# A hybrid decoder layer on one core: where u is scaled, where the SSM answers are split, and when small transfers are issued

## The chip, the core and the metric

The kernel runs on one NeuronCore of a Trainium2 chip. The metric is the device time of one execution in microseconds (us), median of three runs. Engines are named as in the profile: PE (TensorE matmul), PEld (its weight loads), DVE (VectorE), ACT (ScalarE), POOL (GpSimd), SP (SyncE, which here only issues DMAs; SPq and ACTq are the queues of DMA issues on SP and ACT).

## The reference

One decoder layer on x of 2048 tokens by 1024 channels, float32. The input is normalised by RMSNorm and multiplied by one matrix `w_in`; the columns go to three mixers:

- A, sliding-window attention with 4 heads and learned sinks (window 128);
- B, a complex diagonal state space model (SSM, "S5"): 32 groups of 16 channels, 64 complex states a group, a scan over time, then `GELU(Re(C s) + D u)`, then a gated linear unit: `ab = z @ glu_w + glu_b`, `out = ab[:512] * sigmoid(ab[512:])`;
- C, native sparse attention with compressed, selected and window branches.

The three outputs are normalised, projected by `w_out` and added to x; then a feed-forward block `x + w_down @ relu(w_up @ RMSNorm(x))^2` is added.

## The kernel before

Products in float32 precision are made from three fast products: each operand is split into a high word rounded to `fp32r` (an ACT cast) and the rest (a DVE or POOL subtraction), and `mm3` (L80) adds high x high, high x low and low x high in PSUM.

**Stages.** `phase_front` (L93) does the normalisation and `w_in` in two halves of the tokens (8 row tiles each). In each half it first makes `u` for all four 128-channel blocks in two groups of four row tiles (`u_step`, L156), then the column chunks a, b, c (`product`, L170), each with its 8 weight tiles loaded by `load_w` (L153), 2 raw buffers and 12 split ones. Norm factors are not known when the products start: `row_sum` (L112) loads x row-wise and sums squares; `row_factors` (L117) makes 1/rms in `rx` and **stores the [128 x 8] tile transposed to DRAM (`rx_d`, L121)**: 1024 single 4-byte values. In half 0 the front also computes the SSM's parameter tables (`ssm_tables`, L327, a generator run in steps: `TABLE_PARTS = (8, 4)`; its second block, L432 on, loads C, B and D into a pool that opens after the first one has closed) and stores per-pair tables (`pair_steps`). In half 1 the SSM itself is interleaved with the products of a, b, c (`ssm_steps`, L551): for each of 16 pairs of groups it loads u and tables (`loaded`, two pairs ahead), multiplies u by the row factors of both halves (`scaled`, one DVE product of 128x512), multiplies, scans (`scanned`) and answers (`answer`), where GELU leaves `z`; ACT casts it (L627), POOL subtracts (L628), and both words are stored (`stored`, L630).

**Order.** The front is placed by the framework's scheduler: each engine's list is ordered by program order as a priority among what the scheduler thinks ready, and on the chip each engine and each DMA queue runs its list in order. After the front, the local stage and all that follows are ordered by a planner in the kernel (`Flow`, L878): tasks ask for an engine with an estimated duration and a rank, and the planner writes the lists.

**Local stage.** Sliding-window attention (`Local`) runs at high rank; the GLU's 16 row tiles (`glu_tasks`, L2073) run at low rank beside it. For a row tile, `rows_of` (L707) loads both words of z in four DMAs of 128 KB, three tiles ahead (`ZBUFS`); `part` multiplies. The GLU's bias rows are fetched by a task `bias` (L2131) on SP in the planner's order, then cast by ACT (L699) and split by DVE (L703).

Of the kernel before, what the change touches and what calls it, by code (L numbers as in the profile page):

```python
# [92 lines left out]
def phase_front(tc, C, x, norm1_g, w_in, uT, pd, rh_a, prm, ssm_d, rx_d, consts, extra, later, x_t, r_last, last_bank):  # L93

    nc = tc.nc
    with ExitStack() as ctx:
# [56 lines left out]
        def load_w(half, kind, c0, n):  # L153
            return [keep_w(half, kind, c0, n, k, fetch_w(half, kind, c0, n, k, sp, 2, nc.sync)) for k in range(NK)]

        def u_step(half, j, k, hs, w, banks, pool):  # L156
            hh, hl = hs
            for f in range(4):
# [39 lines left out]
        for half in range(2):  # L198
# [10 lines left out]
            if half:  # L209
                tables = table_steps(tc, C, S, ctx.enter_context(tc.tile_pool(name="sgt", bufs=1, side="right", reuse_waits="tile")), ps_t)  # L210
            c_x = ctx.enter_context(ExitStack())
            with tc.tile_pool(name=f"a_psu{half}", bufs=1, space=PSUM, reuse_waits="tile") as ps_u:
                xp = c_x.enter_context(tc.tile_pool(name=f"a_x{half}", bufs=3, **({} if half else {"reuse_waits": "tile"})))
                c_o = ctx.enter_context(ExitStack())
                box_x[:] = [xp, c_o.enter_context(tc.tile_pool(name=f"a_o{half}", bufs=4, side="right", reuse_waits="tile"))]
                banks, parts = {}, []
# [22 lines left out]
                if half == 0:  # L239
# [5 lines left out]
                    run(merge(second, sums[0], [lambda: next(gen)] * TABLE_PARTS[0]))  # L245
# [3 lines left out]
            if half == 0:  # L249
                with tc.tile_pool(name="sg_ps0", bufs=1, space=PSUM, reuse_waits="tile") as ps_g:  # L250
                    l2 = lists[0]
# [75 lines left out]
def ssm_tables(tc, C, S, pool, prm, dkp):  # L327
# [20 lines left out]
    with ExitStack() as ctx:  # L348
        tp = ctx.enter_context(tc.tile_pool(name="si", bufs=1))
        sc = tmp([P, 2, 11, G], "sc")  # L350
        sn, cs = sc[:, 0], sc[:, 1]

        ar, ai, ldt = tmp([P, G], "ar"), tmp([P, G], "ai"), tmp([P, G], "ldt")
        nc.sync.dma_start(ldt, log_dt[0:1].to_broadcast([P, G]))
        for src, dst in ((a_re, ar), (a_im, ai)):
            for j in range(2):
                nc.sync.dma_start(dst[64 * j:64 * j + 64], src)
        dt = exp_acc(nc, tp, ldt, [P, G], "e1")

        yield  # L360
        jt = C["ramp"]
        xr = tmp([P, 17, G], "xr")
        adr, adi = tmp([P, G], "adr"), tmp([P, G], "adi")
        nc.vector.tensor_tensor(adr, ar, dt, op=ALU.mult)
        nc.vector.tensor_tensor(adi, ai, dt, op=ALU.mult)
        nc.vector.tensor_tensor(xr, adr.unsqueeze(1).broadcast_to([P, 17, G]), jt.unsqueeze(2).broadcast_to([P, 17, G]), op=ALU.mult)
        yield
        rho = exp_acc(nc, tp, xr, [P, 17, G], "e2")
        yield
        nc.vector.tensor_copy(rho16, rho[:, 16])  # L370
        yield
        th = tmp([P, 11, G], "th")
        for j in range(11):
            nc.vector.tensor_scalar(th[:, j], adi, float(2 ** j), None, op0=ALU.mult)
        sincos(nc, tp, sc, th, [P, 11, G], "sc")

        yield
        pr, pi_ = (tp.tile([P, 17, G], F32, tag="e2" + n, name="t_p" + n) for n in ("xc", "r"))
        t1, t2 = tmp([P, 8, G], "t1"), tmp([P, 8, G], "t2")
        nc.vector.memset(pr[:, 0], 1.0)  # L380
        nc.vector.memset(pi_[:, 0], 0.0)
        for j in range(4):
            n = 2 ** j
            er = cs[:, j:j + 1].broadcast_to([P, n, G])
            ei = sn[:, j:j + 1].broadcast_to([P, n, G])
            nc.vector.tensor_tensor(t1[:, :n], pr[:, :n], er, op=ALU.mult)
            nc.vector.tensor_tensor(t2[:, :n], pi_[:, :n], ei, op=ALU.mult)
            nc.vector.tensor_tensor(pr[:, n:2 * n], t1[:, :n], t2[:, :n], op=ALU.subtract)
            nc.vector.tensor_tensor(t1[:, :n], pr[:, :n], ei, op=ALU.mult)
            nc.vector.tensor_tensor(t2[:, :n], pi_[:, :n], er, op=ALU.mult)  # L390
            nc.vector.tensor_tensor(pi_[:, n:2 * n], t1[:, :n], t2[:, :n], op=ALU.add)
        nc.vector.tensor_copy(pr[:, 16], cs[:, 4])
        nc.vector.tensor_copy(pi_[:, 16], sn[:, 4])
        nc.vector.tensor_tensor(AR, pr, rho, op=ALU.mult)
        nc.vector.tensor_tensor(AI, pi_, rho, op=ALU.mult)
# [554 lines left out]
def cast_ns(n):  # L950
    return 197 + 0.72 * n
# [1971 lines left out]
```

## Time and profile before

| | us |
|---|---|
| median of 3 runs (2460.09 to 2462.77) | 2462.41 |
| the profiled execution: time | 2462.57 |
| the profiled execution: span | 2460.8 |

The span is what the trace shows; 1.8 us lie around it. PE is busy 96% of the span. A number such as "x85" is a count of instructions; in a list of waits, "idle" is the time that an engine stood just before an instruction, and the name behind the arrow is what ended it. PEclk is the granted TensorE clock as a share of its upper level: 1.00 is 2.4 GHz, 0.50 is 1.2 GHz, and a value between is a mix over the stretch.

### The profile page before, as it was taken

The numbers are of one execution on the slowest core, as the hardware profiler recorded it, in microseconds if no ns is written. First come the engines' busy times: TensorE is split into PE (matmuls) and PEld (weight loads), VectorE is DVE, ScalarE is ACT, GpSimd is POOL, SyncE is SP. The second block draws the span as 40 slices with busy tenths as digits, with TensorE's granted clock in tenths as the row PEclk, the third lists the DMA queues.
The fourth block names the chain that finished last, engine by engine and source line by source line (L and its number), as shares of the span: only waits on it lengthen the run. The fifth ranks groups of instructions, "written<-read, shape, count | busy, mean of one in ns | idle before, by whom it ended". The sixth has DMA issues, their size and how long they took to land. (4 is left out here: it accounts for less than half of the span.)

```text
span 2460.8 us, 37124 instructions
## 1 busy us (share of the span) xinstructions
PE 2367.4 (96%) x12290; PEld 2027.0 (82%) x12290; DVE 1775.2 (72%) x3463; ACT 1302.2 (53%) x2736; POOL 1048.5 (43%) x1080
## 2 busy tenths in 40 slices
PE   8799989799899999999999999999999999999999
PEld 6788989687788888888888888888887888888887
DVE  7764894675687788888665556745558888889886
ACT  5344444675677667666565556444444444434442
POOL 0000243232334345331667664665563544455547
PEclk9799999899999999999999999999999999999999
DMA  8466555563322243210657668654548443444435
GB/s 250 130 216 186 182 180 176 127 214 106 104 87 83 70 123 117 70 54 33 214 182 210 188 193 257 191 155 146 161 146 283 130 125 106 125 133 133 130 99 196
DMA packets 432529, 369.71 MB, mean 150 GB/s; under 512 B 47014, under 2 KB 387244, under 8 KB 430256
## 3 DMA queue, kind: packets, MB, share of 16 engines
q1 hardware_dynamic: 376912, 325.50, 43.6%
q10 hardware_dynamic: 55424, 41.84, 5.4%
q8 instruction: 97, 1.59, 0.3%
q14 instruction: 96, 0.79, 0.1%
HBM read 240.11 MB, written 132.35 MB: 151 GB/s over the span
## 5 line engine op out<-in xcount | busy, mean ns | idle before, releaser
L2180 ACT CAST v<-vr 128x512 fp32r<-128x512 f32 x224 | 139.2, 623 | 303.7 <-DMA vr<-vd 147.0
L2181 DVE TENSOR_TENSOR v<-vr,v 128x512 fp32r<-128x512 f32 x224 | 234.9, 1056 | 76.5 <-ACT v L2180 75.3
L2344 DVE TENSOR_TENSOR ul<-fs,uh 128x512 fp32r<-128x512 f32 x124 | 113.4, 934 | 109.1 <-ACT uh L2343 109.1
L2642 PE MATMUL pdc<-dw,v 128*128 128x512 f32 x768 | 186.4, 392 | 5.2 <-ACT dw L2180 3.9
L2642 PE MATMUL pdb<-dw,v 128*128 128x512 f32 x768 | 184.5, 389 | 0.0
L2642 PE MATMUL pda<-dw,v 128*128 128x512 f32 x768 | 184.5, 389 | 0.0
L2642 PEld LDWEIGHTS pdc<-dw,v 128*128 128x128 f32 x768 | 144.8, 189 | 36.7 <-ACT dw L2180 4.3
L2642 PEld LDWEIGHTS pdb<-dw,v 128*128 128x128 f32 x768 | 144.1, 188 | 30.0
L2642 PEld LDWEIGHTS pda<-dw,v 128*128 128x128 f32 x768 | 144.1, 188 | 29.9
L613 POOL TENSOR_TENSOR t<-Q,E 128x508 f32<-128x508 f32 x16 | 24.5, 1532 | 334.7 <-DMA CA<-dca 273.1
L2343 ACT CAST uh<-fs 128x512 fp32r<-128x512 f32 x124 | 74.4, 620 | 162.3 <-POOL fs L2332 132.6
L2344 DVE TENSOR_TENSOR ul<-ur,uh 128x512 fp32r<-128x512 f32 x93 | 88.7, 955 | 67.9 <-ACT uh L2343 66.4
L2491 POOL TENSOR_TENSOR ev<-ex,e 128x512 f32<-128x512 f32 x32 | 43.2, 1349 | 209.4 <-ACT ex L2474 209.4
L1611 ACT CAST ths<-pps 128x512 fp32r<-128x512 f32 (+1 forms) x144 | 79.2, 562 | 72.4 <-PE pps L1595 63.3
L2474 ACT ACTIVATE e<-e 128x512 f32<-128x512 f32 x128 | 81.0, 633 | 62.3 <-DVE e L2443 60.3
L1938 PE MATMUL pw<-wo_h,mh 128*128 128x512 f32 x256 | 106.6, 416 | 3.2 <-DVE mx L1960 3.1
L1616 DVE TENSOR_TENSOR tls<-pps,ths 128x512 fp32r<-128x512 f32 (+1 forms) x144 | 93.0, 657 | 20.9 <-ACT ths L1611 19.4
L1938 PE MATMUL pw<-wo_l,mh 128*128 128x512 f32 x256 | 104.0, 406 | 0.0
L1938 PE MATMUL pw<-wo_h,ml 128*128 128x512 f32 x256 | 103.9, 406 | 0.0
L2422 PE MATMUL pub<-fh,uh 128*128 128x512 f32 x256 | 100.9, 394 | 1.4 <-ACT uh L2343 0.8
L2422 PE MATMUL puc<-fl,uh 128*128 128x512 f32 x256 | 99.7, 389 | 1.3 <-DVE fl L2362 1.3
L2422 PE MATMUL puc<-fh,uh 128*128 128x512 f32 x256 | 100.1, 391 | 0.0
(554 smaller groups left out, 7659.2 us busy)
## 6 DMA issues: line engine op xcount, KB each, us to landing
vr<-vd SPq DMA_DIRECT2D x224, 256.0 KB
ur<-in_w_up SPq DMA_DIRECT2D x124, 256.0 KB
vd<-ev SPq DMA_DIRECT2D x96, 256.0 KB
vd<-e ACTq DMA_DIRECT2D x64, 256.0 KB
dr<-in_w_down SPq DMA_DIRECT2D x32, 512.0 KB
x<-in_x SPq DMA_DIRECT2D x16, 512.0 KB
z<-dz SPq DMA_DIRECT2D x64, 128.0 KB
mx<-in_x ACTq DMA_DIRECT2D x32, 256.0 KB
```

The source lines that it names most:

```text
L613: nc.gpsimd.tensor_tensor(t[:, :, :, 0:n], Q[:, :, :, 0:n], e.rearrange("p g j c -> p j g c")[:, :, :, 0:n], op=ALU.mult)
L1611: yield "ACT", cast_ns(n), lambda: nc.scalar.copy(th[:, 0:nb], pt[:, 0:nb])
L1616: t = yield "DVE", sub_ns(n), lambda: nc.vector.tensor_tensor(tl[:, 0:nb], pt[:, 0:nb], th[:, 0:nb], op=ALU.subtract)
L1938: t = yield "PE", mm_ns(512), lambda: nc.tensor.matmul(pw[n], a[half][:, j], b[k][:, sl], start=k == 0 and m == 0, stop=k == NK - 1 and m ...
L2180: nc.scalar.copy(dh, src)
L2181: nc.vector.tensor_tensor(dl, src, dh, op=ALU.subtract)
L2343: yield "ACT", 621, lambda: self.nc.scalar.copy(h, src.tile)
L2344: t = yield "DVE", 900, lambda: self.nc.vector.tensor_tensor(l, src.tile, h, op=ALU.subtract)
L2422: nc.tensor.matmul(banks[b], w[:, j], h[:, j], start=k < 4 and j == 0 and i == 0, stop=j == HALF - 1 and i == 2, skip_group_check=True)
L2474: t = yield "ACT", 640, lambda: nc.scalar.activation(r, r, func)
L2491: t = yield "POOL", 1400, lambda: nc.gpsimd.tensor_tensor(E["v" + q].tile, E[x].tile, E[y].tile, op=op)
L2642: nc.tensor.matmul(bank[b, q], x[:, q, j], y[:, j], start=first and j == 0 and n == 0, stop=j == 1 and n == 2, skip_group_check=True)
```

## The change

- `rx_d` is no longer stored in `row_factors`. Both halves' stores stand, in program order, at the start of half 1. In half 1 the second half's factors are loaded back, spread over all partitions, into `rxb` (512 KB), and `u_step` of half 1 multiplies by it on DVE as u leaves PSUM; in half 0 ACT copies u as before. `scaled` multiplies only the first half (128x256), in place.
- Chunk a's weights of half 0 are loaded during `u`'s second group, before most of what followed in program order.
- `ssm_tables` opens the second pool first and loads C, B, D and writes the zero padding of `dkp` one step earlier.
- SSM pairs are loaded three ahead, with one more buffer.
- z is stored unsplit, one word, in an order in which one DMA loads a row tile; ACT and DVE split it in the local stage (`high`, `low`). `glu_w`'s rows are permuted on the host to the new channel order.
- The bias rows are fetched before the planner starts.

```diff
 def row_factors(half):
-            nc.sync.dma_start(rx_d[half].rearrange("r c -> c r"), rx[:, sl])
 # u_step, last k
+   if half:
+       nc.vector.tensor_tensor(o..., banks[f], box_x[2][:, 4 * j:4 * j + 4]..., op=ALU.mult)
+   else:
        nc.scalar.copy(o.rearrange("p r c -> p (r c)"), banks[f])
 # start of half 1
+   for n in range(2):
+       nc.sync.dma_start(rx_d[n].rearrange("r c -> c r"), rx[:, 8 * n:8 * n + 8])
...
+   rxb = box_x[1].tile([P, TS, P], F32, name="rxb", bufs=1)
+   nc.sync.dma_start(rxb..., bass.AP(rx_d[1].tensor, rx_d[1].offset, [[0, P], [1, TS * P]]))
 # half 0
-   run(merge(second, sums[0], [lambda: next(gen)] * TABLE_PARTS[0]))
+   run(merge(second, sums[0], [lambda: next(gen)] * TABLE_PARTS[0],
+             [lambda: box.update({chunks[0]: load_w(0, *chunks[0], range(HALF))})]))
+   box[chunks[0]] += load_w(0, *chunks[0], range(HALF, NK))
 def scaled(b):
-   nc.vector.tensor_tensor(U, raw, rxu..., op=ALU.mult)          # both halves
+   U = M["b", b][0][:, :, 0]
+   nc.vector.tensor_tensor(U, U, rxu.unsqueeze(1)..., op=ALU.mult)
 def answer(b):
-   nc.scalar.activation(z, py, AF.Gelu_apprx_tanh)
-   nc.scalar.copy(zz[:, :, :, 0], z)
-   nc.gpsimd.tensor_tensor(zz[:, :, :, 1], z, zz[:, :, :, 0], op=ALU.subtract)
+   nc.scalar.activation(z.rearrange("p k g c -> p g k c"), py, AF.Gelu_apprx_tanh)
 def rows_of(t):
-   for f in range(4):
-       nc.sync.dma_start(z[:, f]..., zv[t // TS, t % TS, 8 * f:8 * f + 8])
+   nc.sync.dma_start(z, zv[t // TS, t % TS])
+def high(t):  nc.scalar.copy(zh, raws["z", t])
+def low(t):   nc.vector.tensor_tensor(zl, raws.pop(("z", t)), zh, op=ALU.subtract)
 # glu_rows
+   yield "ACT", cast_ns(512), lambda: glu_high(t)
+   s = yield "DVE", sub_ns(512), lambda: glu_low(t)
 # bias(n)
-   t = yield "SP", 50, lambda: steps["bias_fetch"](n)
-   yield landed(flow, t, 4e3)
 # trunk, after near.ahead()
+   for n in (1, 0):
+       g_steps["bias_fetch"](n)
```

## Rows read from the trace of the kernel before

**Rows 1.** The page: busy time by engine, and busy tenths in 40 slices of 61.5 us.
```profile
PE 2367.4 (96%) x12290; PEld 2027.0 (82%) x12290; DVE 1775.2 (72%) x3463; ACT 1302.2 (53%) x2736; POOL 1048.5 (43%) x1080
PE   8799989799899999999999999999999999999999
```
**Rows 2.** Busy time by stage: us from start, length, busy time (x instructions) of each engine, PEclk, DMA share, GB/s. Front half 0: u, then chunks; front half 1: u, then chunks with the SSM; the turn to the local stage; local stage; the rest.
```profile
0.00:53.17 53.17, 46.27 (x193) 37.96 (x193) 40.90 (x125) 33.44 (x53) 0.20 (x4) 1.00 0.87 285
53.17:205.33 152.16, 132.23 (x653) 120.63 (x652) 93.70 (x233) 59.77 (x114) 0.00 (x0) 0.90 0.58 174
205.33:250.45 45.12, 45.12 (x206) 37.38 (x206) 22.75 (x40) 17.47 (x28) 0.00 (x0) 1.00 0.51 151
250.45:430.23 179.78, 164.63 (x1014) 159.42 (x1014) 136.41 (x267) 84.50 (x178) 64.16 (x52) 0.97 0.58 183
430.23:443.39 13.16, 0.85 (x7) 0.41 (x5) 4.27 (x9) 4.42 (x10) 1.99 (x2) 0.71 0.38 126
443.39:647.50 204.11, 193.27 (x1181) 166.50 (x1182) 138.28 (x445) 135.22 (x439) 55.78 (x77) 0.98 0.47 135
```
**Rows 3.** Timelines of SP, ACT and PE around the first store of the row factors (start us, us, engine, line, operation, count, and the idle time before with its releaser).
```profile
51.94 0.38 SPq L121 DMA_DIRECT2D rx_d<-rx  x1
52.42 0.51 SPq L141 DMA_DIRECT2D wr_a<-in_w_in  x1
64.09 0.61 ACT L149 ACTIVATE wh_a<-wr_a,g 128x384 fp32r<-128x384 f32 x1 [9.11 <-DMA wr_a<-in_w_in]
64.76 0.69 PE L82 MATMUL pm_a<-wh_a,hh 128*128 128x384 f32 x1 [7.76 <-ACT wh_a L149]
```
**Rows 4.** The same around the second store, on SP, DVE and PE.
```profile
89.25 0.37 SPq L121 DMA_DIRECT2D rx_d<-rx  x1
92.09 0.59 SPq L444 DMA_DIRECT2D t_B<-in_ssm_b_re  x1
93.41 0.43 SPq L467 DMA_DIRECT2D dkp<-t_zz  x1
102.18 0.69 DVE L452 TENSOR_TENSOR t_v<-t_B,k_qr 128x512 f32<-128x512 f32 x1 [8.12 <-DMA t_B<-in_ssm_b_im]
108.52 0.69 PE L83 MATMUL pm_b<-wl_b,hh 128*128 128x384 f32 x1 [8.78 <-DVE wl_b L150]
```
**Rows 5.** Busy time of the stretches after the two stalls (columns as in rows 2), and two products of chunk b at the upper clock, 24 matmuls apart.
```profile
64.76:70.40 5.64, 5.64 (x17) 5.28 (x18) 5.33 (x18) 3.03 (x6) 0.00 (x0) 0.50 1.09 367
108.52:125.20 16.68, 14.98 (x38) 11.15 (x39) 13.14 (x28) 4.02 (x8) 0.00 (x0) 0.50 0.29 90
152.58 1.02 PE L497 MATMUL pk<-oCA,k_Y 128*128 128x256 f32 x4
157.61 1.02 PE L497 MATMUL pk<-oCA,k_Y 128*128 128x256 f32 x4
```
**Rows 6.** The SP timeline where a transfer of half 1 (r2w, in program order behind half 1's u) is issued; two of its four.
```profile
146.08 0.53 SPq L768 DMA_DIRECT2D r2w<-r  x1
204.63 0.66 SPq L768 DMA_DIRECT2D r2w<-r  x1
```
**Rows 7.** What PE waited for from 250 to 431 us (us in total, times, longest).
```profile
PE py L623 <- POOL St L614: 10.9, 5, 3.4
PE pv L601 <- DVE m L604: 2.5, 2, 1.6
PE pbt L545 <- DVE Bp L541: 0.8, 1, 0.8
PE pv L601 <- DVE U L587: 0.6, 1, 0.6
PE pm_c L83 <- DVE wl_c L150: 0.2, 1, 0.2
```
**Rows 8.** Busy time from 260 to 385 us (columns as in rows 2); POOL's list at the longest of those waits; groups of POOL and DVE from 255 to 420 us (count, busy us, mean ns, idle before).
```profile
260.00:385.00 125.00, 112.52 (x699) 108.00 (x698) 118.15 (x223) 60.29 (x128) 46.17 (x35) 0.96 0.57 179
313.12 1.79 POOL L613 TENSOR_TENSOR t<-Q,E 128x508 f32<-128x508 f32 x1 [7.52 <-DMA Wc<-dkp]
314.87 1.71 POOL L628 TENSOR_TENSOR zz<-zz 128x512 fp32r<-128x512 f32 x1
316.54 0.90 POOL L614 TENSOR_TENSOR St<-t 128x254 f32<-128x254 f32 x1
L628 POOL TENSOR_TENSOR zz<-zz 128x512 fp32r<-128x512 f32 x16 | 23.0, 1440 | 22.7 <-ACT zz L627 22.7
L530 DVE TENSOR_TENSOR t2u<-k_Ea,k_Eb 128x256 f32<-128x256 f32 x24 | 16.7, 695 | 0.5
L532 DVE TENSOR_TENSOR E<-t2u 128x256 f32<-128x256 f32 x24 | 10.5, 437 | 0.5
L587 DVE TENSOR_TENSOR U<-Ur,rxu 128x512 f32<-128x512 f32 x16 | 13.0, 813 | 1.3 <-PE py L621 0.7 <-DMA Ur<-uT 0.5
L604 DVE TENSOR_TENSOR m<-pv,E 128x256 f32<-128x256 f32 x16 | 6.7, 418 | 3.7 <-ACT m L593 3.7
```
**Rows 9.** u's copy out of PSUM on ACT, and a DVE subtraction of the same size out of PSUM: duration ns min/median/max, first and last start.
```profile
L165 ACT COPY uo<-pu x16: 566/587/595, 29.6 to 251.1; 128x512 f32<-128x512 f32 x16
L1616 DVE TENSOR_TENSOR tls<-pps,ths x144: 411/686/694, 628.5 to 1174.4; 128x512 fp32r<-128x512 f32 x128, 128x256 fp32r<-128x256 f32 x16
```
**Rows 10.** Timelines of SP, ACT and PE at the turn to the local stage, and the stretch after it (columns as in rows 2).
```profile
425.16 11.19 SPq L710 DMA_DIRECT2D z<-dz  x12
436.39 1.06 SPq L694 DMA_DIRECT2D gbr<-in_glu_b  x2
440.80 1.25 ACT L699 CAST glu_bh<-gbr 1x512 fp32r<-1x512 f32 x2 [8.65 <-DMA gbr<-in_glu_b]
442.22 0.47 ACT L1067 ACTIVATE wa<-ptka,gains 128x256 fp32r<-128x256 f32 x1
443.39 0.47 PE L1108 MATMUL pqa<-wa,qAa 128*128 128x128 f32 x1 [10.13 <-DVE wa L1068]
443.39:450.40 7.01, 7.01 (x26) 6.00 (x27) 4.01 (x17) 5.07 (x15) 0.00 (x0) 0.57 0.15 37
```
**Rows 11.** A cast and a subtraction of 128x512 in the local stage and in the up-projection: group rows (busy us, mean ns, idle before).
```profile
L1154 ACT CAST tha<-ppa 128x512 fp32r<-128x512 f32 x30 | 17.2, 581 | 2.3 <-PE ppa L1147 2.2
L1158 DVE TENSOR_TENSOR tla<-ppa,tha 128x512 fp32r<-128x512 f32 x30 | 20.2, 683 | 2.3 <-ACT tha L1154 2.2
L2344 DVE TENSOR_TENSOR ul<-ur,uh 128x512 fp32r<-128x512 f32 x93 | 88.7, 955 | 67.9 <-ACT uh L2343 66.4
```

More of the change, by code (lines that the diff above doesn't have):

```diff
@@ L151, in keep_w, with load_w @@
             return wh, wl
-        def load_w(half, kind, c0, n):
-            return [keep_w(half, kind, c0, n, k, fetch_w(half, kind, c0, n, k, sp, 2, nc.sync)) for k in range(NK)]
+        def load_w(half, kind, c0, n, ks=range(NK)):
+            return [keep_w(half, kind, c0, n, k, fetch_w(half, kind, c0, n, k, sp, 2, nc.sync)) for k in ks]
         def u_step(half, j, k, hs, w, banks, pool):
@@ L215, in phase_front @@
                 box_x[:] = [xp, c_o.enter_context(tc.tile_pool(name=f"a_o{half}", bufs=4, side="right", reuse_waits="tile"))]
+                if half:
+                    rxb = box_x[1].tile([P, TS, P], F32, name="rxb", bufs=1)
+                    box_x.append(rxb)
+                    nc.sync.dma_start(rxb.rearrange("p r c -> p (r c)"), bass.AP(rx_d[1].tensor, rx_d[1].offset, [[0, P], [1, TS * P]]))
                 banks, parts = {}, []
@@ L567, in factors @@
     def factors():
-        for h in range(2):
-            src = rx_d[h]
-            nc.sync.dma_start(rxu[:, h], bass.AP(src.tensor, src.offset, [[P, TS], [0, 16], [1, P]]))
+        src = rx_d[0]
+        nc.sync.dma_start(rxu, bass.AP(src.tensor, src.offset, [[P, TS], [0, 16], [1, P]]))
     def loaded(b):
-        raw, CA, Wc = tl([P, GB, 2, P], "Ur", b, 2), tl([P, GB, 17, 16], "CA", b, 3), tl([P, GB, 256], "Wc", b, 3)
+        U, CA, Wc = tl([P, GB, 2, P], "U", b, 4), tl([P, GB, 17, 16], "CA", b, 4), tl([P, GB, 256], "Wc", b, 4)
         for i in range(GB):
             g = b * GB + i
-            nc.sync.dma_start(raw[:, i].rearrange("p h c -> p (h c)"), uT[16 * g:16 * g + 16].rearrange("q r h c -> r q (h c)"))
+            nc.sync.dma_start(U[:, i].rearrange("p h c -> p (h c)"), uT[16 * g:16 * g + 16].rearrange("q r h c -> r q (h c)"))
         nc.sync.dma_start(CA, dr["ca"][b])
@@ L707, in rows_of, with high, low @@
     def rows_of(t):
-        z = sp.tile([P, 4, 2, P], F32R, tag="z", name=f"z{t}", bufs=ZBUFS)
-        for f in range(4):
-            nc.sync.dma_start(z[:, f].bitcast(F32).rearrange("p l c -> p (l c)"), zv[t // TS, t % TS, 8 * f:8 * f + 8])
-        box[t] = [z]
+        z = raws["z", t] = sp.tile([P, 4, P], F32, tag="z", name=f"z{t}", bufs=ZBUFS)
+        nc.sync.dma_start(z, zv[t // TS, t % TS])
+    def high(t):
+        zh = sp.tile([P, 4, P], F32R, tag="zh", name=f"zh{t}")
+        zl = sp.tile([P, 4, P], F32R, tag="zl", name=f"zl{t}")
+        box[t] = [zh, zl]
+        nc.scalar.copy(zh, raws["z", t])
+    def low(t):
+        zh, zl = box[t]
+        nc.vector.tensor_tensor(zl, raws.pop(("z", t)), zh, op=ALU.subtract)
     def bank(tag, name):
@@ L743, in glu_steps @@
     return ahead, ps, dict(fetch=fetch, zeroed=zeroed, load_high=load_high, load_low=load_low, bias_fetch=bias_fetch, bias_high=bias_high, bias_low=bias_low), (
-        rows_of, bank, part, last, gate, gated, square, store)
+        rows_of, bank, high, low, part, last, gate, gated, square, store)
 def bias_vectors(tc, tp, ps, rel_bias, oh2, ohs, r2, rs):
```

245 lines of the change are left out of this document (124 added, 121 removed).

## The prediction

> **What bounds the kernel now.** I read the page first, then the stages, then PE's waits stage by stage, and last the timelines on both sides of each long wait. PE is busy 96% of the span [rows 1], and the slices that fall below 9 all lie in the first 700 us; after that PE is full and nothing of this change runs. So the change can only win back PE's idle time and the time that PE spent at the lower clock, and only up to about 650 us. The stages show how much there is [rows 2]: half 0's chunks have 152.2 us for 132.2 us of PE work, at a mean clock of 0.90; half 1's u is full; half 1's chunks with the SSM have 179.8 us for 164.6; the turn to the local stage is 13.2 us with 0.9 us of work; the local stage has 204.1 us for 193.3.
>
> Four places make up nearly all of it.
>
> *First store of the row factors.* SP issues it at 51.94 us; the last weight tile of chunk a is issued 0.5 us later and reaches ACT only at 64.09, 11.7 us after its issue. PE stands 7.76 us [rows 3] and then runs 5.64 us at 0.50 [rows 5].
>
> *Second store.* Issued at 89.25; the four loads of B behind it arrive at 102.18, 10.1 us after the last issue. DVE stands 8.12 us at its first use of B, the split of chunk b's weights is queued behind it on DVE, and PE stands 8.78 us [rows 4]. The next 16.7 us run wholly at the lower clock [rows 5].
>
> *SSM stage.* PE waits 15.0 us in ten waits, 10.9 of them for POOL's state `St` [rows 7]. From 260 to 385 us DVE is busy 118.2 of 125 us [rows 8]: it is the second bound there.
>
> *Turn to the local stage.* Twelve z loads hold SP from 425.16 to 436.39, the bias rows are issued behind them, ACT stands 8.65 us for them, attention's window cast is queued behind that on ACT, and PE stands 10.13 us [rows 10].
>
> **The change part by part.** All terms are of the profiled execution, 2462.57 us (span 2460.8 and 1.8 around it); the median of the runs shown is 2462.41, so no correction is needed.
>
> *1. Chunk a's last weights.* Without a store in front, the loads issue earlier and the 7.76 us wait goes. The slow stretch goes with it: at the upper clock a product of 24 matmuls and a table group of 4 take 5.03 us, from 152.58 to 157.61 [rows 5], 0.18 us a record, so its 17 records need 3.1 us, not 5.64: 2.6 us. Bounds 0 and 10.4. C, B, D and the padding of `dkp` now come ahead too, about 0.8 MB at the 285 GB/s of that stage [rows 2], under 3 us of transfer, and chunk a's tiles have moved up more than that. I take 10.
>
> *2. Parameters first.* DVE no longer meets B late, which frees the 8.78 us; the slow stretch behind it has 38 records, 6.8 us of work in 16.68, so 9.8 us more are at stake. But the stretch also holds waits of its own, table products that need DVE, bias products that ACT must empty, and chunk b's last two weight tiles, which need two buffers of chunk a to come free. Bounds 0 and 18.6; I take 11.
>
> *3. The two stores, wherever they go.* They remain two transfers of 1024 values of 4 bytes, and whatever is queued on SP behind one waits: 11.7 and 10.1 us from issue to arrival [rows 3, 4]. If nobody needs what is behind them, they cost nothing; if PE needs it both times, 21.8. Program order puts them behind all of half 0, but the scheduler fills SP: `r2w`, which in program order stands behind half 1's u, was issued at 146.08 for its first copy and only at 204.63 for its last [rows 6]. So the stores will fall somewhere between 55 and 200 us, into chunk b or c, where weight tiles have two raw buffers and little slack. I take a loss of 4, nearer the lower end because each store hits at most one or two tiles.
>
> The Trainium skill (DMA: Bandwidth & Descriptors, Rules for kernel authors) says that a non-contiguous last dimension makes one descriptor per element. By that rule the stores would cost the same in any place, which is rival A. The same page (Specifications) says that pieces under 512 B are read, modified and written back, which speaks against moving the `dkp` padding forward too, since its pieces are 448 B; in the trace it was issued at 93.41, behind B [rows 4], so no row isolates it. By that rule the first term would lose some of its 10 us, and the sum would be nearer 2433.
>
> *4. u scaled on DVE in half 1.* Eight copies move from ACT (0.587) to DVE (0.686 for the like shape out of PSUM) [rows 9], 5.5 us more on DVE in a stage where it is busy 22.8 of 45.1 us [rows 2]; PE's banks come free 0.1 us later each, 0.8 in all. The eight stores of u are issued from ACT's queue and now wait for DVE; nothing PE needs soon is behind them. The new load `rxb` (512 KB, 1.8 us at 285 GB/s) must be there when u's first group ends; it can be issued some 20 us before. Cost 0, bounds 0 and 4.
>
> *5. SSM stage.* POOL loses 16 subtractions of 1.44 us. One of them stood between POOL's two steps towards `St` in the longest wait, 1.71 of 3.4 us [rows 7, 8]. ACT loses 16 casts. DVE loses half of `scaled`: 16 times 0.813 less about 0.418 (the 128x256 row of `m`), 6.3 us. DVE also runs slower beside POOL: `t2u` has a mean of 0.695 where `E` of the same shape has 0.437 [rows 8]; with 23 of POOL's 62 us gone I expect a few us of that back. The stage has 15.0 us of waits and a clock of 0.97, that is 6% of 179.8 us at half rate, 5.4 us: 20.4 at most. The wait next in line is the chain pv, ACT, DVE, scan, ACT, POOL itself, which stays. Bounds -20.4 and +3 (the scheduler will order the lists anew); I take 9 gained.
>
> *6. The turn.* The bias rows arrive before they are needed, and SP issues 3 z loads instead of 12. What is late next is attention's window: 1.17 us from ACT's cast at 442.22 to PE at 443.39 [rows 10], so at most 9.0 us go; with the bias casts (1.25 us each pair) possibly still ahead on ACT I take 7.5. After the wait PE ran 7.01 us at 0.57, which lost 3.0; a shorter wait may still bring the clock down, so I take 1.5.
>
> *7. Splitting z in the local stage.* 16 casts of 0.581 on ACT and 16 subtractions of 0.683 on DVE [rows 11], 9.3 and 10.9 us, enter a stage where ACT is busy 135 and DVE 138 of 204 us [rows 2]. The GLU is PE's filler, so most is hidden; attention's short steps queue behind some of them. Bounds 0 and 20.2 (all on the path); I take 3. SP's 48 fewer issues (11.19/12 = 0.93 us each) gain nothing after the turn.
>
> Where POOL works beside DVE a subtraction of the same shape with both operands in SBUF took 0.955 [rows 11]. The Trainium skill (GPSIMD Engine Reference, Key points) says why: GpSimd shares its SBUF interfaces with VectorE, and instructions with two SBUF inputs contend. By that rule the new splits would take 15.3 us of DVE instead of 10.9, and term 5 would gain from the same cause; the sum would hardly move.
>
> *Sum:* half 0: 10 + 11 - 4 = 17; SSM stage 9; local stage 7.5 + 1.5 - 3 = 6. Together 32: 2462.57 - 32 = 2430.6, said as 2430.
>
> **Rivals.**
>
> *A. The stores stay where they were.* The scheduler issues each as soon as its factors are ready, in a pause of SP, as it issued the first `r2w` [rows 6]. For it: SP has pauses around both places. Against: the last `r2w` waited 58 us longer, so lower priority does delay. Then term 1 is half won (5), term 2 only as far as DVE no longer waits for B while chunk b's last tiles still come late (4), and no further loss is booked: 9 + 9 + 6 = 24, 2439.
>
> *B. All of it goes.* 10.4 + 18.6 + 20.4 + 9.0 + 3.0 = 61.4: 2401. For it: the causes are few and each is touched. Against: the stretches behind the stalls hold waits of other engines.
>
> *C. DVE stays the bound.* With DVE at 118 of 125 us [rows 8] the SSM stage gains nothing, and the splits cost 9 in the local stage: 17 + 0 + 0 = 17, 2446. For it: DVE gets u's scaling and the splits. Against: it loses 6.3 us just where it was full.
>
> *D. Slower: the stores meet the turn of the halves.* If both stand in SP's list directly before half 1's u, with `rxb` behind them, x, u's weights and `rxb` wait 21.8 us, PE stands for that and runs 2.6 to 9.8 us slow afterwards [rows 5], and `rxb` adds some 3: about 31. If also terms 2 and 5 bring only 4 and 0, the gains are 10.4 + 4 + 6 = 20.4, and the time is 2473. It decides from a stall of 20 us on if those gains are all; against the forecast's gains (36 without term 3) it would need 36. Against it: half 1's first loads were spread over 50 us before they were needed, and the stores are ready from 52 and 89 us on.
>
> **How the numbers follow.** Forecast (2420 to 2438) 45%, A 21%, B 13%, C 13%, D 5%, an outcome within the bound of no change 3%. The range 2408 to 2450 holds the forecast, A and C and the nearer part of B, and leaves out the rest of B and D, under 2 in 10. A difference of 0.2% (4.9 us) is about what a measurement of this kernel tells from none. Faster by more: 92%; within: 3%; slower: 5%.
>
> **What would show it.** Right: no wait of PE above 3 us between 53 and 205 us (before's times); half 0's chunks shorter by 15 to 20 us; DVE not standing for B; POOL's list in the SSM stage with two operations a pair and PE's waits for `St` halved; PE's wait at the turn under 4 us, with ACT not standing for the bias. Wrong: a new wait of 5 us or more for a weight or x tile issued just behind an `rx_d` store (A, D), PE waiting for u's banks or `rxb`, PE waiting on DVE for z's low word, or DVE still above 94% from 260 to 385 us with waits unchanged (C).

## The result, and where the time went

The changed kernel takes 2437.3 us (median of 4 runs, 2436.96 to 2438.39), the kernel before, timed beside it, 2461.25 (4 runs): ratio 0.9907, with a 95% interval of 0.9890 to 0.9924. That is 24 us faster. The forecast was 2430, its own range 2420 to 2438, the whole range given 2408 to 2450.

The total hides what matters: the stages gained other amounts than the prediction gave them. The table marks stages by PE's products in the two traces: half 0 runs from the last product of half 0's u to the first of half 1's, the SSM stage from the last product of u to the last of chunk c, the turn from there to attention's first product, the local stage from there to the GLU's last product, the rest to the last product of all.

| stage | before, us | after, us | gain | forecast |
|---|---|---|---|---|
| half 0 (terms 1 to 3) | 152.8 | 150.3 | 2.5 | 17 |
| u of half 1 (term 4) | 44.3 | 44.3 | 0 | 0 |
| SSM stage (term 5) | 179.9 | 168.0 | 11.9 | 9 |
| turn (term 6) | 13.9 | 6.3 | 7.6 | 7.5, and 1.5 of clock |
| local stage (term 7) | 203.3 | 206.4 | -3.1 | -3 |
| the rest | 1806.1 | 1800.8 | 5.3 | 0 |

With 0.9 before the first mark it sums to 25.1. Half 0, which was to bring more than half of the gain, brought next to nothing. Two things hid that in part: a larger gain in the SSM stage, and 5 us in the rest, where nothing was changed.

The page of the changed kernel, beside [rows 1]:

```profile
PE 2359.3 (97%) x12290; PEld 2020.4 (83%) x12290; DVE 1777.3 (73%) x3486; ACT 1298.3 (53%) x2728; POOL 1024.1 (42%) x1065
PE   8799999999899999999999999999999999999999
```

Busy time by stage in the changed kernel, beside [rows 2] (start and end, length, busy time of PE, PEld, DVE, ACT and POOL with their instructions, PEclk, DMA share, GB/s): u, half 0, u of half 1, SSM stage, turn, local stage.

```profile
0.00:52.30 52.30, 45.27 (x192) 37.25 (x193) 37.31 (x111) 31.60 (x49) 0.39 (x5) 1.00 0.88 268
52.30:201.94 149.64, 128.17 (x653) 117.48 (x652) 97.13 (x247) 63.16 (x118) 0.00 (x0) 0.93 0.74 206
201.94:247.04 45.10, 45.10 (x206) 37.38 (x206) 25.59 (x44) 13.57 (x21) 0.00 (x0) 1.00 0.33 93
247.04:414.86 167.82, 161.57 (x1014) 156.24 (x1014) 122.67 (x272) 75.00 (x160) 39.49 (x36) 0.99 0.55 169
414.86:420.52 5.66, 0.85 (x8) 0.40 (x5) 5.25 (x9) 5.53 (x13) 1.99 (x2) 0.96 0.60 176
420.52:627.71 207.19, 195.12 (x1181) 168.07 (x1182) 150.16 (x461) 140.84 (x452) 57.57 (x77) 0.97 0.40 117
```

In half 0 PE does 128 us of work in 150 and stands for 21; in the SSM stage it stands for 6 instead of 15; the turn is 5.7 us long instead of 13.2.

**The first stall stayed, with another cause.** The place that answers to [rows 3] in the changed kernel: SP, ACT, DVE and PE around chunk a's weights.

```profile
47.85 0.43 SPq L439 DMA_DIRECT2D dkp<-t_zz  x1
48.88 2.23 SPq L140 DMA_DIRECT2D wr_a<-in_w_in  x2
67.83 0.99 SPq L140 DMA_DIRECT2D wr_a<-in_w_in  x2
55.78 1.12 ACT L148 ACTIVATE wh_a<-wr_a,g 128x384 fp32r<-128x384 f32 x2 [0.44 <-ACT uo L167]
67.09 0.18 DVE L456 TENSOR_TENSOR k_qi<-k_qi,t_den 128x32 f32<-128x32 f32 x1
67.19 0.61 DVE L149 SCALAR_TENSOR_TENSOR wl_a<-wr_a,g,wh_a 128x384 fp32r<-128x384 f32 x1
67.86 0.69 PE L83 MATMUL pm_a<-wl_a,hh 128*128 128x384 f32 x1 [10.78 <-DVE wl_a L149]
```

No row-factor store is near, and still PE stands for 10.78 us (7.76 in [rows 3]). The tiles were there: ACT casts two of them at 55.78 and had waited for ACT's own work, not for a DMA. DVE's split of the first comes only at 67.19, directly behind `k_qi` of the SSM's tables. SP can issue the last two tiles only at 67.83, since their two raw buffers are free when DVE has split. What DVE did in those 10.8 us:

```profile
57.07:67.86 10.79, 0.01 (x2) 0.01 (x1) 10.41 (x46) 2.30 (x4) 0.00 (x0) 0.71 0.31 96
```

DVE was busy for 10.41 of 10.79 us, with 46 instructions: 44 of table work and the splits of the two tiles. In the kernel before the split stood first in DVE's list, and the tables stood still behind it until its tile came:

```profile
64.74 0.62 DVE L150 SCALAR_TENSOR_TENSOR wl_a<-wr_a,g,wh_a 128x384 fp32r<-128x384 f32 x1 [8.28 <-ACT wh_a L149]
```

Now the splits are placed behind the tables, which run ahead of what PE waits for. It is the order that does this and not the parameters that now come first: of the 44 only two (L465, which reads B, and L477, which reads D) use any of them.

**The stores took their stall along.** SP, ACT and PE where the first store stands now, and the 10 us behind it as a stretch (columns as above):

```profile
102.62 0.39 SPq L213 DMA_DIRECT2D rx_d<-rx  x1
104.26 0.36 SPq L140 DMA_DIRECT2D wr_b<-in_w_in  x1
115.81 0.61 ACT L148 ACTIVATE wh_b<-wr_b,g 128x384 fp32r<-128x384 f32 x1 [7.66 <-DMA wr_b<-in_w_in]
116.48 0.69 PE L82 MATMUL pm_b<-wh_b,hh 128*128 128x384 f32 x1 [5.82 <-ACT wh_b L148]
```

```profile
104.00:114.00 10.00, 6.66 (x35) 5.44 (x33) 4.19 (x18) 2.48 (x5) 0.00 (x0) 0.94 0.59 38
116.48:125.00 8.52, 8.26 (x29) 7.35 (x30) 6.21 (x14) 1.97 (x4) 0.00 (x0) 0.61 0.90 176
```

Chunk b's tile issued 1.6 us behind the store reaches ACT 11.5 us later. In that time the DMA engines are busy for 0.59 of the time and move 38 GB/s, where half 0 has 206 in the mean. PE stands 5.82 us and then runs 8.5 us at a mean of 0.61 of the upper clock.

### The profile page after: what moved, and what is told of

Same layout as the page of the kernel before. It is cut to its first block, busy times and chain, and to the rows that moved or that the text cites. A ratio compares the mean times of both kernels' runs of the same rounds, so it can differ in the third digit from the quotient of the medians.

```text
span 2435.6 us, 37090 instructions
## 1 busy us (share of the span) xinstructions
PE 2359.3 (97%) x12290; PEld 2020.4 (83%) x12290; DVE 1777.3 (73%) x3486; ACT 1298.3 (53%) x2728; POOL 1024.1 (42%) x1065
## 5 line engine op out<-in xcount | busy, mean ns | idle before, releaser
L2359 ACT CAST uh<-fs 128x512 fp32r<-128x512 f32 x124 | 74.4, 620 | 159.0 <-POOL fs L2348 128.6
L2507 POOL TENSOR_TENSOR ev<-ex,e 128x512 f32<-128x512 f32 x32 | 43.1, 1347 | 204.9 <-ACT ex L2490 204.9
```

What stands on the lines that cost most here:

```text
L2359: yield "ACT", 621, lambda: self.nc.scalar.copy(h, src.tile)
L2507: t = yield "POOL", 1400, lambda: nc.gpsimd.tensor_tensor(E["v" + q].tile, E[x].tile, E[y].tile, op=op)
```

## The experiments

Each was timed beside the kernel before, and its ratio is to that; the stages are those of the first table, from one trace of each kernel.

| kernel | median, us | ratio, 95% | half 0 | SSM | turn | local | rest |
|---|---|---|---|---|---|---|---|
| changed kernel | 2437.3 | 0.9890 to 0.9924 | 150.3 | 168.0 | 6.3 | 206.4 | 1800.8 |
| e4: before, stores later | 2460.2 | 0.9987 to 1.0008 | 151.9 | 181.7 | 14.1 | 204.8 | 1804.3 |
| e9: before, stores as rows | 2444.6 | 0.9915 to 0.9953 | 136.5 | 181.0 | 14.1 | 204.2 | 1806.1 |
| e1: padding late | 2424.9 | 0.9844 to 0.9878 | 138.6 | 166.7 | 6.3 | 205.6 | 1801.6 |
| e5: padding from POOL | 2437.3 | 0.9873 to 0.9914 | 148.4 | 167.6 | 6.4 | 206.0 | 1802.3 |
| e2: stores as rows | 2423.3 | 0.9839 to 0.9868 | 136.0 | 168.5 | 6.4 | 203.3 | 1801.2 |
| e3: e1 and e2 | 2416.3 | 0.9809 to 0.9838 | 128.3 | 166.8 | 6.3 | 205.2 | 1803.0 |
| e10: e2, parameters at old step | 2419.0 | 0.9802 to 0.9861 | 128.6 | 167.0 | 6.3 | 204.8 | 1801.8 |
| e6: before, z unsplit | 2446.2 | 0.9900 to 0.9947 | 152.3 | 172.8 | 7.3 | 205.7 | 1802.0 |
| e7: u's scaling undone | 2440.2 | 0.9887 to 0.9928 | 152.5 | 169.4 | 5.1 | 208.4 | 1800.8 |
| e8: before, bias rows early | 2454.7 | 0.9956 to 0.9979 | 148.4 | 180.3 | 5.1 | 209.0 | 1802.3 |
| e11: two pairs ahead | 2443.1 | 0.9915 to 0.9948 | 149.8 | 173.5 | 6.4 | 203.3 | 1803.4 |

A stage that an edit doesn't touch shows what one trace is worth: the kernel before, e6 and e8 have half 0 in common and took 152.8, 152.3 and 148.4 for it; the kernels built on the changed one with its SSM stage (the changed kernel, e1, e2, e3, e5 and e10) took 166.7 to 168.5 for that.

### The stores alone, moved or made cheap (e4, e9)

Here only the place of the stores changes, in the kernel before.

```diff
 def row_factors(half):
-            nc.sync.dma_start(rx_d[half].rearrange("r c -> c r"), rx[:, sl])
 # start of half 1
+                for n in range(2):
+                    nc.sync.dma_start(rx_d[n].rearrange("r c -> c r"), rx[:, 8 * n:8 * n + 8])
```

> The kernel before with one edit only: both stores of the row factors in program order at the start of half 1. By the prediction's terms 1 to 3 (10 + 11 - 4): 2445, with chunk a's wait of 7.8 us and DVE's wait of 8.1 us for B gone. Rival (the stores take their stall along wherever they are issued): 2455 to 2462, with a PE wait of 5 us or more for a tile just behind a store.

It measured 2460.2, no change. The two stalls of before are gone, and others of the same size have come. What PE waited for between 50 and 206 us (total, times, longest), and the place of the first store:

```profile
PE pk L498 <- ACT kst L502: 11.1, 2, 7.4
PE pm_a L82 <- ACT po_a L181: 8.9, 2, 6.6
```

```profile
61.37 0.38 SPq L210 DMA_DIRECT2D rx_d<-rx  x1
62.67 4.04 SPq L140 DMA_DIRECT2D wr_b<-in_w_in  x4
75.05 0.61 ACT L148 ACTIVATE wh_b<-wr_b,g 128x384 fp32r<-128x384 f32 x1 [9.01 <-DMA wr_b<-in_w_in]
```

ACT stands 9 us for the tile behind the store, and its emptying of PE's bank (`po_a`) is queued behind that cast: 6.6 of PE's 8.9 us. The victim is another engine's work; the price is of the same size. The 7.4 us of `kst` come 26 us after the second store (issued at 135.96); that it made them is not shown.

In the kernel before, too, the store is made otherwise, in its old place in the program:

```diff
-            nc.sync.dma_start(rx_d[half].rearrange("r c -> c r"), rx[:, sl])
+            pt = ps_t.tile([P, 512], F32, tag="pt", name=f"prx{half}")
+            nc.tensor.transpose(pt[0:8, 0:P], rx[:, sl], C["ident"])
+            rxT = sm.tile([8, P], F32, tag="rxT", name=f"rxT{half}", bufs=2)
+            nc.vector.tensor_copy(rxT, pt[0:8, 0:P])
+            nc.sync.dma_start(rx_d[half], rxT)
```

> The kernel before with one edit only: each half's row factors are turned by a PE transpose where they are made, and stored as 8 rows of 512 B instead of 1024 single values. Theory (the single values alone made both stalls of half 0): PE's waits of 7.8 us in chunk a and 8.8 us in chunk b go, half 0 from u's end to half 1's u gets 15 to 22 us shorter, time 2439 to 2447. Rival (B arrives late and the table work is late with it, store or not): half 0 at most 8 us shorter, 2452 to 2460.

Half 0 took 136.5 us, 16.3 less than in the kernel before, and the time 2444.6: inside what the theory gave. The first store, the stretch behind it, SP's own queue in that stretch (packets, MB, share of 16 engines), and the longest wait of PE that is left in half 0:

```profile
56.74 0.35 SPq L125 DMA_DIRECT2D rx_d<-rxT  x1
```

```profile
57.00:62.00 5.00, 4.28 (x24) 4.28 (x25) 4.73 (x18) 2.48 (x5) 0.00 (x0) 1.00 1.07 329
q1 hardware_dynamic: 372, 0.63, 39.4%
```

```profile
PE pk L501 <- ACT kst L505: 3.8, 1, 3.8
```

For comparison, the 10 us behind the first store in the kernel before:

```profile
53.00:63.00 10.00, 4.00 (x23) 3.64 (x21) 3.33 (x14) 1.99 (x4) 0.00 (x0) 0.86 0.49 27
```

The same 4 KB, in 8 pieces instead of 1024: SP's queue moves 0.63 MB in 5 us behind it, 126 GB/s (the rest of the 329 comes from ACT's queue), where it moved 27 before. Only the first store shows the shape by itself, at 56.74 where it was at 51.94: the scheduler put the second at 148.34, 59 us later than before. B still arrives late in this kernel (its loads issue at 82.2), and DVE does not stand for it.

### Chunk a's stall: order on DVE, or the padding's transfer (e1, e5)

e1 takes the padding's store out of `ssm_tables` and puts it at the start of `pair_steps`; e5 leaves it where it is and issues it from POOL.

```diff
 # e1, in pair_steps
+    def padding():
+        zz = tp.tile([16, 112], F32, name="t_zz", bufs=1)
+        nc.gpsimd.memset(zz, 0.0)
+        nc.sync.dma_start(dr["k"][:, :, 0:112].rearrange("g q c -> q g c"), zz...)
+    res = [lambda: None] * 5 + [padding]
 # e5
-            nc.sync.dma_start(dkp[:, :, 0:112].rearrange("g q c -> q g c"), zz...)
+            nc.gpsimd.dma_start(dkp[:, :, 0:112].rearrange("g q c -> q g c"), zz...)
```

> The changed kernel with the zero padding of dkp stored at the start of the pair tables; all other parameter loads stay early. In the scheduler's list the splits of chunk a's weight tiles 4 to 7 then stand ahead of most table operations on DVE. Theory (order on DVE makes the stall of chunk a): PE's wait of 10.8 us in chunk a falls to 2 us or less, nothing new stalls where the padding is issued now (in front of chunk b's last tiles), time 2424 to 2430. Rival (the padding's own transfer holds up the queue): the stall moves with the padding, 8 us or more for a weight tile of chunk b behind it, time 2434 to 2440.

> The changed kernel with one edit: the zero padding of dkp is issued from POOL's queue instead of SP's, at the same point of the program and so at about the same time; every other transfer stays on SP. The scheduler's list then has chunk a's splits early on DVE. Theory (order on DVE): chunk a's wait of 10.8 us falls to 2 us or less though the padding's 512 pieces still move beside the weight tiles; half 0 about 8 us shorter, time 2426 to 2432. Rival (the padding's transfer itself delays the tiles): a wait of 6 us or more for a weight tile stays in chunk a, time 2434 to 2440.

e1 measured 2424.9: chunk a's waits for the splits are 1.8 us in three, and PE waits for no tile of chunk b, in front of whose last tiles the padding is issued now (90.56). But chunk b's stall of 5.82 us is gone as well, though e1 still stores single values in half 0. Where the stores stand in e1, a weight tile issued behind the second and its cast on ACT, and the 10 us behind each store:

```profile
63.48 0.43 SPq L213 DMA_DIRECT2D rx_d<-rx  x1
122.76 0.43 SPq L213 DMA_DIRECT2D rx_d<-rx  x1
127.44 0.87 SPq L140 DMA_DIRECT2D wr_c<-in_w_in  x2
138.10 0.63 ACT L148 ACTIVATE wh_c<-wr_c,g 128x396 fp32r<-128x396 f32 x1 [7.45 <-DMA wr_c<-in_w_in]
```

```profile
64.00:74.00 10.00, 10.00 (x53) 10.00 (x52) 7.59 (x31) 6.19 (x13) 0.00 (x0) 0.88 0.94 156
123.00:133.00 10.00, 10.00 (x57) 9.69 (x56) 6.30 (x13) 4.14 (x8) 0.00 (x0) 1.00 1.23 102
```

The tile behind the second store still takes 10.7 us to reach ACT, and ACT stands 7.45 us, but PE works through both stretches without a pause; its only wait in the 20 us behind either store is one of 1.41 us, at 78.27. So the gain of e1 (11.7 us in half 0) is not chunk a's stall alone, and a store of single values costs PE only what PE soon needs behind it.

e5 lost chunk a's stall too, and gained nothing in all. What PE waited for in e5, two of SP's issues, and one of PE's products:

```profile
PE bpr L773 <- DMA boh<-in_k_oh: 10.4, 2, 9.3
PE pm_a L83 <- DVE wl_a L149: 1.6, 2, 1.3
```

```profile
98.04 0.37 SPq L213 DMA_DIRECT2D rx_d<-rx  x1
98.51 0.47 SPq L771 DMA_DIRECT2D boh<-in_k_oh  x1
109.71 1.59 PE L773 MATMUL bpr<-boh,tab 33*8 33x432 f32 x2 [9.33 <-DMA boh<-in_k_oh]
```

The scheduler placed the stores elsewhere in this list (64.0 and 98.0), and behind the second stood a tile that PE wanted: 9.33 us, the gain given back. e5 is weaker against its rival than I had meant: POOL issued the padding at 22.5 us, long before chunk a's tiles, so the transfers did not run side by side. It does show the padding's own size:

```profile
dkp<-t_zz POOLq DMA_DIRECT2D x1, 224.0 KB, 4.6
```

4.6 us from issue to landing. Together with the changed kernel's rows (tiles present at 55.78, DVE busy for 10.41 of 10.79 us) the order on DVE is shown as the cause. Why the scheduler chose that order is not shown; moving the padding alone was enough to change it.

### Both causes away, and what the early parameters are worth (e2, e3, e10)

In the changed kernel both halves' factors are turned at once and stored as rows (e2); with e1's edit as well (e3); or with B, D and the padding at their old step (e10). The one store of rows then stands at 189.2 (e2), 180.9 (e3) and 182.4 (e10), at the end of half 0: these three show half 0 without a store of factors among its chunks, and do not part the store's shape from its place.

```diff
-                for n in range(2):
-                    nc.sync.dma_start(rx_d[n].rearrange("r c -> c r"), rx[:, 8 * n:8 * n + 8])
+                pt = ps_t.tile([P, 512], F32, tag="pt", name="prx")
+                nc.tensor.transpose(pt[0:NT, 0:P], rx, C["ident"])
+                rxT = sm.tile([NT, P], F32, tag="rxT", name="rxT", bufs=1)
+                nc.vector.tensor_copy(rxT, pt[0:NT, 0:P])
+                nc.sync.dma_start(rx_d.rearrange("h r c -> (h r) c"), rxT)
```

> The changed kernel with both halves' row factors turned by one PE transpose and stored as 16 rows of 512 B instead of 2 times 1024 single values. Theory (the single values make the queue stand): PE's wait of 5.8 us at 110 us and the slow stretch after it go, chunk a's wait of 10.8 us stays; time 2427 to 2432. Rival (the tiles behind the store wait for free buffers, not for the store): the wait stays within 2 us of 5.8 and the time within 3 us of 2437.

> Both edits of the two runs before: padding with the pair tables, row factors stored as rows. Theory: the two stalls are independent and both go, no wait of PE above 3 us from 52 us to the start of half 1's u; half 0 gets 17 us shorter than in the changed kernel at most, time 2414 to 2422. Rival (DVE's work on the tables is the bound of half 0 and only shows elsewhere): not more than 6 us below the better of the two, 2424 to 2430.

> The changed kernel with the row factors stored as rows and with B, D and the padding back at their old step of the tables. Theory (loading the parameters first is worth little once the stores are cheap): no stall above 3 us in half 0, time within 5 us of the run with rows and late padding, 2411 to 2422. Rival (the early parameters are worth the 11 us of term 2): DVE stands for B and PE behind it, 2425 or more.

e2: 2423.3, more than the theory gave (2427 to 2432), since chunk a's wait was 7.0 us in this trace and 10.8 in the changed kernel, with the same instructions on DVE up to there. e3: 2416.3, and half 0 is 22 us shorter than in the changed kernel, where e1 and e2 alone gave 11.7 and 14.3. Since e1 was already rid of both stalls, e3's further 10.3 us are something else: PE stands 3.8 us there instead of 11.2, and e1's longest single wait is 2.5; which part of that the stores made is not shown. e10: 2419.0, with a ratio (0.9831) inside e3's interval. Half 0 of e1 and of e3 as a stretch, the longest wait of PE that e10 has in half 0, and e10's first load of B:

```profile
52.50:190.80 138.30, 127.12 (x656) 116.08 (x655) 94.40 (x246) 60.83 (x118) 0.44 (x1) 0.98 0.75 202
52.50:180.30 127.80, 124.02 (x655) 114.80 (x654) 93.17 (x236) 60.69 (x116) 0.44 (x1) 0.99 0.70 216
```

```profile
PE bpr L776 <- DVE tab L768: 3.4, 1, 3.4
```

```profile
41.98 0.47 SPq L454 DMA_DIRECT2D t_B<-in_ssm_b_re  x1
```

In e3 PE works 124 of 127.8 us at a clock of 0.99; there is little left here. e10 is not the test that it was meant to be: at their old step in the program B's loads still issue at 41.98, where the changed kernel has them at 41.72 and the kernel before at 90.28; the pool that they need opens first here too. So it shows only that the step itself does not matter. Half 0 is 8 us longer in e9 (B late) than in e3 and e10 (B early); how much of that is B, and how much chunk a's earlier weights, no run separates. e3 beats both kernels by a clear margin: 21 us under the changed one.

### The SSM stage and the turn (e6, e7, e11, e8)

e6 puts z's part alone into the kernel before (unsplit store, split in the local stage, one load a row). e7 undoes u's scaling in the changed kernel, e11 its third pair ahead. e8 puts the early bias rows alone into the kernel before.

```diff
 # e7, u_step and scaled
-                        nc.vector.tensor_tensor(o..., banks[f], box_x[2][:, 4 * j:4 * j + 4]..., op=ALU.mult)
+                    nc.scalar.copy(o.rearrange("p r c -> p (r c)"), banks[f])
-        nc.vector.tensor_tensor(U, U, rxu.unsqueeze(1).broadcast_to([P, GB, P]), op=ALU.mult)
+        nc.vector.tensor_tensor(U, U, rxu.unsqueeze(1).broadcast_to([P, GB, 2, P]), op=ALU.mult)
 # e11, ssm_steps, with three buffers of U, CA and Wc
-                lambda b=b: (b and stored(b - 1), b + 3 < NB and loaded(b + 3))]
+                lambda b=b: (b and stored(b - 1), b + 2 < NB and loaded(b + 2))]
 # e8, trunk, after near.ahead(), and the fetch in bias(n) taken out
+                for n in (1, 0):
+                    g_steps["bias_fetch"](n)
```

> The kernel before with one part alone: z stored unsplit and split in the local stage. Theory (POOL's subtraction between its two steps made PE wait for St): the SSM stage of 179.9 us gets 8 to 12 us shorter, PE's waits for St fall from 10.9 us to 5 or less; the turn gets 5 to 7 us shorter too, since the bias rows stand behind 3 z loads instead of 12; the local stage loses 2 to 5; time 2442 to 2450. Rival (DVE is the bound of the SSM stage, and only the halved scaling relieves it): SSM stage within 4 us of before, time 2451 to 2458.

> The changed kernel with u's scaling undone: ACT copies u in both halves, both halves are multiplied in the SSM stage (128x512 instead of 128x256), rxb is not loaded. By the forecast (term 4 zero; 6.3 us of DVE that do not bound the stage once POOL has less to do): SSM stage 0 to 4 us longer than in the changed kernel, time 2436 to 2442. Rival (DVE bounds the stage): 6 us longer or more, 2443 to 2450.

> The changed kernel with the SSM pairs loaded two ahead instead of three, with three buffers each. From the runs before, by subtraction: z alone made the SSM stage 7 us shorter, z with the third pair ahead 10.5, so the third pair would be worth 3.4. Theory: SSM stage 171 us (168.0 in the changed kernel), with PE or DVE waiting for U or Wc out of DRAM; time 2438 to 2443. Rival (the 3.4 us are what one list of the scheduler differs from another): SSM stage within 1 us of 168, time within 3 us of the changed kernel's.

> The kernel before with one part alone: the bias rows are fetched before the planner starts. By the forecast's term 6: PE's wait of 10.1 us at the turn falls below 4 us and the time by 7 to 9 us, 2450 to 2453. Rival (the twelve z loads and casts stand there anyway): the wait stays above 7 us, 2456 to 2461.

PE's waits for `St` in the changed kernel, e6 and e7 (one fence each), to be held against the 10.9 us of [rows 7]; then DVE's waits for U in the changed kernel and in e11; and PE's wait at the turn in e8, against the 10.13 of [rows 10].

```profile
PE py L630 <- POOL St L621: 3.5, 3, 1.6
```

```profile
PE py L623 <- POOL St L614: 9.3, 5, 2.3
```

```profile
PE py L624 <- POOL St L615: 7.3, 5, 2.0
```

```profile
DVE U L595 <- DMA U<-uT: 7.4, 7, 2.0
```

```profile
DVE U L595 <- DMA U<-uT: 12.7, 7, 4.3
```

```profile
PE pqa L1108 <- DVE wa L1068: 1.3, 1, 1.3
```

e6 measured 2446.2, inside what was expected, but half of its reason fell. The SSM stage got 7.1 us shorter, yet the waits for `St` only went from 10.9 to 9.3. Its stretch says where the rest is:

```profile
249.44:422.20 172.76, 161.51 (x1014) 156.68 (x1013) 125.06 (x268) 75.71 (x163) 41.29 (x36) 0.99 0.55 167
```

PE's busy time fell from 164.63 [rows 2] to 161.51 at a clock of 0.99 instead of 0.97: 3.1 us of the gain is the same work at a higher clock. The other 4 are waits; those for `m` and `Bp` (3.3 us in [rows 7]) are gone.

e7 measured 2440.2 with an SSM stage of 169.4, 0.9 to 2.7 us longer than in the kernels that share the changed one's: u's scaling halves PE's waits for `St` (7.3 to 3.5) and is still worth little by itself, as forecast. e11 measured 2443.1, 5.8 above the changed kernel, and its SSM stage is 5.5 longer: the third pair ahead, which the prediction never priced, is by these traces the second largest part of the stage's gain. e8 measured 2454.7, 8.2 less than the kernel before timed beside it (2462.88). Its turn is 8.8 shorter, but its local stage 5.7 longer, so the two together give 3.1 (4.5 in the changed kernel); its half 0 and its rest, which the edit does not touch, are 4.4 and 3.8 shorter. So the stages bear the 8.2 out only roughly. e6 alone has 6.6 of the turn too, since its bias rows stand behind three z loads instead of twelve: the two parts win the same wait, once.

## Why the time fell into the range, and which of the reasons held

The time lies at the upper edge of the forecast's own range: 24 of the 32 us were gained. Half 0 fell short by 14.5, and 2.9 more in the SSM stage with 5.3 in the rest, which nobody forecast, made up for part of it; that is luck. The total is nearer to rival A's 2439 than to 2430, though A's reason did not come either. In half 0 the prediction's own signs spoke against it: "no wait of PE above 3 us between 53 and 205 us" was to show it right, and 10.78 and 5.82 came; "a new wait of 5 us or more for a weight or x tile issued just behind an `rx_d` store" was to show it wrong, and the 5.82 is one.

- **Term 1 (10 us, chunk a).** Wrong. Without the store in front the tiles came in time, as predicted, and the wait grew from 7.76 to 10.78 us. The step that failed: "the loads issue earlier and the 7.76 us wait goes". It took a tile's arrival for the end of the wait, and DVE's order, in which the split came first, as given. The new list has nearly 10 us of table work on DVE in front of the splits. e1, with B and D as early as in the changed kernel, and e3 show that the wait goes when the splits stand ahead.
- **Term 2 (11 us, B early).** B did come early, and DVE does not stand for it. What that is worth by itself stays open: in e9 B comes late and DVE does not stand either, so the 8.12 us of [rows 4] came with the store in front of B; what else early loads bring to half 0 no run separates.
- **Term 3 (a loss of 4 from the moved stores).** Mis-sized: "each store hits at most one or two tiles" is true, and one tile is enough. The first cost 5.82 us of waiting and about 3 of clock (8.5 us at 0.61), where the term had 4 for both. With one store of rows at the end of half 0 (e2), half 0 is 14.3 us shorter, of which 3.7 is chunk a's wait in that trace: about 10 for the two. The term's other sentence, "If nobody needs what is behind them, they cost nothing", holds by e1.
- **Terms 1 to 3 together** were 17. In the kernel before, making the stores rows gave 16.3 (e9, where the second also moved), and moving them gave nothing (e4). The Trainium skill (DMA: Bandwidth & Descriptors, Rules for kernel authors) says that a non-contiguous last dimension becomes one descriptor per element, and to rearrange. The prediction had said that by this rule the stores cost the same in any place, tied that to rival A, and gave it 21%. For the queue that came true: what stood behind a store reached its engine 10.1 to 11.7 us after its issue in the kernel before, the changed one, e1 and e5. For PE it did not: 9.33 us of waiting in e5, 5.82 in the changed kernel, 1.41 in e1. Rival A's own mechanism (the scheduler leaves the stores where they were) did not come, for they moved to 102.6 and 119.1.
- **The second rule**, that pieces under 512 B are read, modified and written back (the Trainium skill, the same page, Specifications), would have cost some of term 1. The runs show no price that PE noticed: the padding's 512 pieces landed 4.6 us after issue in e5, and e1 has no stall behind them. What did harm was the padding's place in the program: with it moved, the order on DVE was another.
- **Term 4 (0).** Right: 44.3 us both times; the product took 0.687 us on DVE against the forecast 0.686.
- **Term 5 (9).** Right in size (11.9), incomplete in its parts. z's part gave 7.1, the third pair ahead about 5.5, u's halved scaling about 1, each measured alone or undone in one trace, so they need not add up, and that the sum met the 9 is partly chance. The step named first, POOL's subtraction in PE's waits for `St`, was mis-sized: taking it out alone (e6) took these waits from 10.9 to 9.3, and only with the third pair and u's scaling are they 3.5. Halving `scaled` saved 4.3 us of DVE (16 times 0.813 to 0.546), not 6.3. That DVE runs slower beside POOL holds, but not as a rate: in the kernel before `t2u` and `E` have the same median, 0.426 and 0.424, and 9 of the 24 `t2u` took 0.83 to 1.39; in the changed kernel 5 of 25 took 1.36 to 1.53.
- **Term 6 (7.5 and 1.5).** The wait went as forecast: 7.6 gained at the turn, and PE now waits 2.08 us for `qBa` (2.18 before) and 2.73 for attention's window (10.13), 4.8 together. The 1.5 of clock did not show: the 7 us behind the turn ran at 0.55, where they had 0.57, though the wait was shorter.
- **Term 7 (-3).** The local stage is 3.1 us longer, but the changed kernel and e1, e2, e3, e5, e10 and e11, with the same stage, took 203.3 to 206.4 (mean 204.9), and before, e4 and e9 203.3 to 204.8 (mean 204.1): the splits cost about 1, and the agreement with 3 is chance. The 16 subtractions took 0.807 us in the mean, between the 0.683 that I took and the 0.955 measured beside POOL [rows 11], but none of them took that: 14 took 0.66 to 0.69 and two 1.68, and those two started while POOL was in a TENSOR_TENSOR. One of the two, and `t2u` of the kernel before (ns, min/median/max):

```profile
437.52 1.47 POOL L841 TENSOR_TENSOR qda<-ta,rh_a 128x768 f32<-128x768 f32 x1 [0.53 <-PE ptka L848]
437.86 1.68 DVE L725 TENSOR_TENSOR zl<-z,zh 128x512 fp32r<-128x512 f32 x1
```

```profile
L530 DVE TENSOR_TENSOR t2u<-k_Ea,k_Eb x24: 399/426/1391, 261.7 to 381.9; 128x256 f32<-128x256 f32 x24
```

- **The rest (5.3)** was given as zero. It took 1802.3 to 1806.1 us in before, e4, e8 and e9, and 1800.8 to 1803.4 in the kernels with z's part: up to half of it is spread, and whether the new GLU tasks leave a few us there stays open.
- **Rivals.** B and C did not come. D's mechanism came in small: a store in front of a tile that PE wants, 5.8 us instead of 21.8, in chunk b and not at the turn of the halves.

## What to carry to other kernels

- A small transfer of single values holds what is queued behind it for some 10 us, wherever it stands. What that costs depends on who waits there: 9.33 us of PE in e5, 1.41 for both stores in e1. Where a scheduler picks the place, moving the transfer is a gamble; changing its shape (one transpose of 0.27 us on PE, one copy of 0.28 us on DVE, 8 or 16 rows) takes the hold away.
- When a tile is made to come earlier, ask what else must happen to it, and what stands in front of that in the other engine's list. Here DVE's table work was placed ahead of the splits that PE was waiting for, and the freed stall came back in the same place under another name.
- When a total comes out near the forecast, set the stages side by side before believing the reasons: here a stage that gave 2.5 us instead of 17 was covered in part by two others.

## What had not been expected of the hardware

- Behind 4 KB in 1024 pieces the queue moved 38 GB/s for 10 us (changed kernel, 104 to 114) with the DMA engines only 0.59 busy; behind 4 KB in 8 pieces SP's queue moved 126 GB/s (e9, 57 to 62).
- 512 pieces of 448 B (224 KB), issued from POOL's queue, landed in 4.6 us: half as many pieces, fifty times the bytes, and less than half the time that the tiles behind 1024 single values took to arrive (11.5 us).
- With z's cast and subtraction out of the SSM stage (e6), the same products ran there at a clock of 0.99 instead of 0.97, worth 3 us of its 7; the waits that vanished from PE were each 3.4 us or shorter.
- DVE was not slowed beside POOL by a share but held by single instructions: a subtraction that started 0.34 us into a POOL instruction of 1.47 us took 1.68 us instead of 0.69 and ended 0.55 us after it. All 14 slow `t2u` of the two kernels (0.83 us or more) started while POOL was in an instruction, and none of the others did; three of the other subtractions of z had POOL start within them and still took 0.68.
